# One decoder layer on one core: where the weights lie against the moving rows in two groups of projections, and the order in which the columns are read in a third

## The chip, the core and the metric

The kernel runs on 1 core of one Trainium2 chip (trn2) and is launched once. The metric is the device time of that launch in microseconds. A core has five engines that work side by side: TensorE (PE in the profile, with its weight loads shown apart as PEld), VectorE (DVE), ScalarE (ACT), GpSimd (POOL) and SyncE (SP, which here only starts DMAs). On-chip data lies in SBUF (128 partitions, a long row of bytes in each); a matmul reads both of its operands from SBUF and writes PSUM. Of the two operands, the *stationary* one (here always 128 columns) is loaded first, and the *moving* one (here 256 columns, mostly) is streamed past it.

## The reference

One layer on a sequence of 256 positions with 1024 features, float32 throughout:

```python
proj = x @ w_in + b_in                  # 1024 -> 4*1024 + 8 + 3*1024 + 2*1024 columns
q_m, k_m, v_m, o_m, i_m, f_m, q_b, k_b, v_b, g_a, g_b = split(proj)
q_m, k_m = silu(causal_conv4(q_m, k_m))             # along positions
y_a = sigmoid(o_m) * head_norm(mlstm(q_m, k_m, v_m, i_m, f_m))   # 4 heads x 256
y_b = causal_attention(q_b, k_b, v_b, rel_bias)                  # 8 heads x 128
mix = (sigmoid(g_a) * (y_a @ w_branch_a) + sigmoid(g_b) * (y_b @ w_branch_b)) @ w_out
x = layer_norm(ALPHA * x + mix)
u = causal_conv3(x @ w_up)              # 2 * 2816 columns
x = layer_norm(ALPHA * x + (silu(u_gate) * u_up) @ w_down)
```

## The kernel before

Everything that TensorE multiplies in bulk is float32 split into a high and a low part (type fp32r). A product of two such operands takes three matmuls, `mm3`: high by high, high by low, low by high (lines 125, 126 and 127).

**Steps.** The weights come in 81 chunks of 1 MB (128 partitions by 2048 float32, 8 KB in each partition). `chunk_order` lists them, and the main loop in `run` takes one chunk a step. A step s starts the DMA of chunk s + 5 into a `raw` buffer, splits chunk s + 2 into `wh` and `wl` (`split_into`: a cast on ACT, line 91, and a subtraction on DVE, line 92), and multiplies with chunk s. So the weights of a step are ready two steps ahead, and SyncE's queue holds nothing but the DMAs of chunks and the stores of the output.

**Groups.** Behind four steps for the output gate (`o`) come four groups, 0 to 3, of eight projections each, always in the order qm, qb, km, kb, vm, vb, ga, gb. A projection is one step: 256 columns of `w_in`, 8 slices of 128 in the contraction, 2 halves, 3 matmuls each: 48 matmuls. Between the projections of a group stand the small matmuls of the two branches (their tiles are psw, pss, psl, psn, pst, psy and pso). Then follow `wa`, `wb`, `wo` and the feed-forward part (`up`, `dn`).

**Which operand moves.** In `mm_feat` (qm, qb, km, kb, ga, gb) the weights are stationary, 128 columns at a time, and the 256 positions of x (tiles `xth`, `xtl`: high and low) move. In `mm_tok` (vm, vb, and `o`) it is the other way round: 128 positions of x are stationary, and 256 columns of the weights move.

**Distances.** `wh` and `wl` are views into tiles that are 64 columns wider than the widest chunk needs; `shift` gives the column at which the view begins. "Distance" means here the start of the stationary operand less the start of the moving one, in float32 columns, modulo 64 (256 bytes). The tiles begin at addresses that are equal modulo 512 bytes, and slices follow each other in whole multiples of 128 columns, so a projection has one distance throughout. Before, it is 16 in all 32 projections: the views begin at column 16 where the weights are stationary, at 48 where they move. Three kinds of matmul differ: the very first of each vm, which loads a copy of x with a place of its own (`xfirst`); the first two of the `o` steps (`mm_early`, line 159), which move 512 columns from column 0 of the weight tiles, at distance 0; and the last of the `o` steps (PSUM tiles `ps_o3` and `ps_o3b`), which moves rows of 264 columns (the projection's 256 and 8 for the mLSTM gates), so that the distance falls by 8 from slice to slice and takes each multiple of 8 once.

**Results.** `ps` is a PSUM tile of 2 x 256 columns, which ACT and DVE read in the next step; nothing in this reading depends on the order in which TensorE wrote the columns.

Of the kernel before, what the change touches and what calls it, by code (L numbers as in the profile page):

```python
# [21 lines left out]
KT = D // P  # L22
# [35 lines left out]
    return order  # L58


def shift(kind):

    if kind in ("vm", "vb", "o"):
        return 48
    if kind in ("wa", "wb"):
        return 56
    return 0 if kind in ("wo", "dn") else 16


class Kernel:  # L70
# [27 lines left out]
    def split_parts(self, s):  # L98
        if s >= len(self.order) or s in self.w:
            return []  # L100
        raw = self.raw.pop(s)
        if s in self.extra:
            wh, wl = self.extra.pop(s)
        else:
            wh = self.stream.tile([P, WCOLS], F32R, tag="wh", name=f"wh{s}", bufs=3)
            wl = self.stream.tile([P, WCOLS], F32R, tag="wl", name=f"wl{s}", bufs=3)
            a = shift(self.order[s][0])
            wh, wl = wh[:, a:a + KT * 264], wl[:, a:a + KT * 264]
        if s == 3:

            vh, vl = (t.rearrange("p (k f) -> p k f", k=KT) for t in (wh, wl))
            vr = raw.rearrange("p (k f) -> p k f", k=KT)
            cuts = [tuple(t[:, 4 * i:4 * i + 4, 0:256] for t in (vh, vl, vr)) for i in range(2)]
            cuts.append((vh[:, :, 256:264], vl[:, :, 256:264], self.wif))
        else:
            wh, wl = wh[:, 0:2048], wl[:, 0:2048]
            cuts = [tuple(t[:, i * 1024:(i + 1) * 1024] for t in (wh, wl, raw)) for i in range(2)]
        self.w[s] = (wh, wl)
        return [lambda c=c: self.split_into(*c) for c in cuts]
# [9 lines left out]
    def mm_feat(self, s, ps, xh, xl, mid=None, first=None):  # L129
        wh, wl = self.w.pop(s)  # L130
        wh = wh.rearrange("p (k f) -> p k f", k=KT)
        wl = wl.rearrange("p (k f) -> p k f", k=KT)
        for j in range(2):
            if j and mid:
                mid()
            c = slice(j * P, (j + 1) * P)
            for k in range(KT):
                self.mm3(ps[:, j, :], wh[:, k, c], wl[:, k, c], xh[:, k, :], xl[:, k, :], k == 0, k == KT - 1,
                         first if j == k == 0 else None)

    def mm_tok(self, w, ps, xh, xl, toks=(0, 1), kouter=False, ks=range(KT), first=None):
        wh, wl = w
# [1034 lines left out]
```

## Time and profile before

| | |
|---|---|
| time, median of 2 runs | 498.08 us (497.45 and 498.71) |
| span of the profiled execution, first to last instruction | 495.6 us |
| its own time outside the span | not listed; the median less the span is 2.5 us |
| TensorE busy, its weight loads busy | 484.4 us (98%), 468.0 us (94%) |
| VectorE, ScalarE, GpSimd busy | 369.2 us (74%), 288.5 us (58%), 29.1 us (6%) |
| groups 1, 2 and 3, first matmul of qm to that of the next group | 49.9 us each |
| mean DMA rate | 189 GB/s |

How to read it: the page of a profile describes one execution. Engine times are sums over its instructions; matmuls overlap each other, so a matmul of 276 ns that starts every 113 ns still makes "busy" no more than the span. Rows name the line of the kernel, the engine, the operation, and output <- inputs with the numbers of buffers left out, so `wh` stands for all of its buffers. In a timeline the first column is the start in us from the span's start and the second the duration.

### The profile page before, as it was taken

How to read it: one execution, taken by the hardware profiler on the slowest of the kernel's cores; microseconds unless marked ns; L12 is line 12 of the kernel's file. 1: busy time of each engine (PE TensorE's matmuls, PEld its weight loads, DVE VectorE, ACT ScalarE, POOL GpSimd, SP SyncE). 2: the span in 40 equal slices, each digit the busy share in tenths (PEclk: the TensorE clock that was granted, in tenths of full speed). 3: DMA queues.
4: the chain of work that ended last, by engine and by line, in shares of the span. 5: the costliest groups of instructions: out<-in, count | busy, mean ns of one | idle time of the engine just before them, and what ended most of it. 6: DMA issues, size and time to landing. Idle time of an engine off the chain costs nothing.

```text
span 495.6 us, 9471 instructions
## 1 busy us (share of the span) xinstructions
PE 484.4 (98%) x3889; PEld 468.0 (94%) x3889; DVE 369.2 (74%) x662; ACT 288.5 (58%) x479; POOL 29.1 (6%) x46
## 2 busy tenths in 40 slices
PE   8999999999999999999999999999999999999992
PEld 4899999999999999999999999999999999999982
DVE  5676995888588858885677788888667766866886
ACT  6567867496658665866655524766554555554610
POOL 0400011001100110002000001000000000000001
PEclk9999999999999999999999999999999999999998
DMA  8984555556554645443945572646555456444202
GB/s 251 351 305 153 202 197 200 175 173 193 184 184 171 196 172 196 172 171 136 371 176 179 221 280 86 255 145 212 203 206 175 165 181 245 170 171 171 86 1 85
DMA packets 19036, 93.74 MB, mean 189 GB/s; under 512 B 4625, under 2 KB 5913, under 8 KB 9009
## 3 DMA queue, kind: packets, MB, share of 16 engines
q1 hardware_dynamic: 14834, 87.08, 49.2%
q0 software_dynamic: 4160, 6.07, 3.9%
q8 instruction: 30, 0.49, 0.4%
q14 instruction: 12, 0.10, 0.1%
HBM read 92.05 MB, written 2.63 MB: 191 GB/s over the span
## 4 chain that ended last, share of the span: by engine, by line
PE 94%; DMA 2%; DVE 1%; SPq 1%; ACT 0%; issue 0%; POOL 0%; POOLq 0%
PE ps_up L127 8%; PE ps_up L126 8%; PE ps_up L125 8%; PE ffn L127 4%; PE ffn L126 4%; PE ffn L125 4%; PE ps_vm L125 2%; PE ps_vm L127 2%; PE ps_qm L125 2%; PE ps_vm L126 2%; PE ps_ga L127 1%; PE ps_ga L125 1%; PE ps_vb L126 1%; PE ps_vb L127 1%; PE ps_vb L125 1%; PE ps_ga L126 1%
## 5 line engine op out<-in xcount | busy, mean ns | idle before, releaser
L92 DVE TENSOR_TENSOR wl<-raw,wh 128x1024 fp32r<-128x1024 f32 (+1 forms) x162 | 187.5, 1197 | 29.2 <-ACT wh L91 29.0
L91 ACT CAST wh<-raw 128x1024 fp32r<-128x1024 f32 (+1 forms) x162 | 158.8, 1030 | 11.6 <-DMA raw<-in_wst_dram 6.3
L127 PE MATMUL ps_up<-x1h,wl 128*128 128x256 f32 x320 | 89.9, 281 | 0.0
L126 PE MATMUL ps_up<-x1l,wh 128*128 128x256 f32 x320 | 89.9, 281 | 0.0
L125 PE MATMUL ps_up<-x1h,wh 128*128 128x256 f32 x319 | 89.7, 281 | 0.0
L126 PEld LDWEIGHTS ps_up<-x1l,wh 128*128 128x128 f32 x320 | 61.4, 192 | 0.0
L127 PEld LDWEIGHTS ps_up<-x1h,wl 128*128 128x128 f32 x320 | 60.1, 188 | 0.0
L125 PEld LDWEIGHTS ps_up<-x1h,wh 128*128 128x128 f32 x319 | 59.9, 188 | 0.0
L1010 DVE SCALAR_TENSOR_TENSOR cu<-ps_up,vec,cu 128x255 f32<-128x255 f32 (+1 forms) x80 | 33.0, 475 | 27.1 <-ACT cu L1006 26.9
L127 PE MATMUL ffn<-wh,hl 128*128 128x512 f32 (+1 forms) x110 | 38.4, 349 | 0.0
L126 PE MATMUL ffn<-wl,hh 128*128 128x512 f32 (+1 forms) x110 | 38.4, 349 | 0.0
L125 PE MATMUL ffn<-wh,hh 128*128 128x512 f32 (+1 forms) x110 | 38.3, 349 | 0.0
L91 ACT CAST hh<-cu 128x256 fp32r<-128x256 f32 x22 | 8.9, 407 | 42.8 <-DVE cu L1018 42.8
L1006 ACT ACTIVATE cu<-ps_up,vec 128x256 f32<-128x256 f32 x40 | 16.8, 472 | 28.8 <-PE ps_up L127 28.0
L126 PEld LDWEIGHTS ffn<-wl,hh 128*128 128x128 f32 x110 | 20.8, 189 | 3.0
L125 PEld LDWEIGHTS ffn<-wh,hh 128*128 128x128 f32 x110 | 20.7, 188 | 3.0
L127 PEld LDWEIGHTS ffn<-wh,hl 128*128 128x128 f32 x110 | 20.7, 188 | 2.9
L125 PE MATMUL ps_gb<-xth,wh 128*128 128x256 f32 x64 | 18.0, 282 | 0.0
L126 PE MATMUL ps_vm<-wl,xth 128*128 128x256 f32 x64 | 17.9, 280 | 0.0
L127 PE MATMUL ps_vm<-wh,xtl 128*128 128x256 f32 x64 | 17.9, 280 | 0.0
L125 PE MATMUL mix<-wh,mgh 128*128 128x256 f32 x64 | 17.8, 279 | 0.0
L125 PE MATMUL ps_qm<-xth,wh 128*128 128x256 f32 x64 | 17.8, 278 | 0.0
(295 smaller groups left out, 1428.9 us busy)
## 6 DMA issues: line engine op xcount, KB each, us to landing
raw<-in_wst_dram SPq DMA_DIRECT2D x78, 1024.0 KB, 4.9
raw<-in_wst_dram SPq DMA_DIRECT2D x8, 256.0 KB, 4.5
lnrow<-in_rows_dram POOLq DMA_DIRECT2D x4, 512.0 KB, 7.5
band<-table POOLq DMA_DIRECT2D x4, 384.0 KB, 13.0
xraw<-in_xt_dram SPq DMA_DIRECT2D x8, 128.0 KB, 4.3
raw<-in_wst_dram SPq DMA_DIRECT2D x2, 512.0 KB, 7.6
toe<-band POOLq DMA_DIRECT2D x4, 256.0 KB, 4.2
xtok<-in_x_dram POOLq DMA_DIRECT2D x1, 1024.0 KB, 8.3
```

The costliest lines, as they stand in the source:

```text
L91: self.nc.scalar.copy(wh, raw)
L92: self.nc.vector.tensor_sub(wl, raw, wh.bitcast(F32))
L125: mm(ps, ah if first is None else first, bh, start=start, stop=False)
L126: mm(ps, ah, bl, start=False, stop=False)
L127: mm(ps, al, bh, start=False, stop=stop)
L1006: act.activation(cu[:, j, :], ps[:, j, :], AF.Copy, scale=tap(2, j))
L1010: v.scalar_tensor_tensor(cu[:, j, o:], ps[:, j, :S - o], tap(t, j), cu[:, j, o:], op0=ALU.mult, op1=ALU.add)
```

## The change

The change gives `shift` the group as well. In groups 1 and 3 a table sets the column at which each projection's view begins, and so its distance, for both `wh` and `wl`. Worked out as above, the distances after it are:

| | qm | qb | km | kb | vm | vb | ga | gb |
|---|---|---|---|---|---|---|---|---|
| groups 0 and 2 (and all groups before) | 16 | 16 | 16 | 16 | 16 | 16 | 16 | 16 |
| group 1 | 24 | 20 | 12 | 8 | 24 | 12 | 4 | 0 |
| group 3 | 32 | 40 | 48 | 56 | 0 | 56 | 60 | 18 |

In group 2 the six projections of `mm_feat` stay at 16, but the 256 moving columns are streamed in another order, and the PSUM tile is written in the same order, so each result lands where it did. For qm the order is backwards (255, 254, ... 0). For the others the two halves of the 256 columns alternate in blocks: c columns of the first half, c of the second, c of the first, and so on, with c = 16 (qb), 32 (km), 4 (kb), 64 (ga) and 8 (gb). In the built program each is one matmul as before, with another access pattern.

No instruction is added, removed or moved on any engine. What differs on TensorE is the access patterns of group 2 and the addresses in groups 1 and 3; on ACT and DVE it is the addresses to which the splits of groups 1 and 3 write.

```diff
-def shift(kind):
-
+PLACES = {
+    1: {"qm": 24, "qb": 20, "km": 12, "kb": 8, "vm": 40, "vb": 52, "ga": 4, "gb": 0},
+    3: {"qm": 32, "qb": 40, "km": 48, "kb": 56, "vm": 0, "vb": 8, "ga": 60, "gb": 18},
+}
+READS = {"qm": "back", "qb": 16, "km": 32, "kb": 4, "ga": 64, "gb": 8}
+
+
+def shift(kind, i=0):
+
+    if i in PLACES and kind in PLACES[i]:
+        return PLACES[i][kind]
     if kind in ("vm", "vb", "o"):
         return 48
...
-            a = shift(self.order[s][0])
+            a = shift(*self.order[s])
             wh, wl = wh[:, a:a + KT * 264], wl[:, a:a + KT * 264]
...
+        kind, i = self.order[s]
+        how = READS.get(kind) if i == 2 else None
+
+        def seen(t):
+            if how is None:
+                return t
+            if how == "back":
+                return t[:, ::-1]
+            return t.rearrange("p (a b c) -> p b a c", a=2, c=how)
+
         for j in range(2):
...
-                self.mm3(ps[:, j, :], wh[:, k, c], wl[:, k, c], xh[:, k, :], xl[:, k, :], k == 0, k == KT - 1,
-                         first if j == k == 0 else None)
+                self.mm3(seen(ps[:, j, :]), wh[:, k, c], wl[:, k, c], seen(xh[:, k, :]), seen(xl[:, k, :]), k == 0,
+                         k == KT - 1, first if j == k == 0 else None)
```

## The prediction

> **What bounds the kernel now.** The page comes first, for who is busy and what the chain that ended last consists of.
>
> ```profile
> span 495.6 us, 9471 instructions
> ## 1 busy us (share of the span) xinstructions
> PE 484.4 (98%) x3889; PEld 468.0 (94%) x3889; DVE 369.2 (74%) x662; ACT 288.5 (58%) x479; POOL 29.1 (6%) x46
> ...
> PE 94%; DMA 2%; DVE 1%; SPq 1%; ACT 0%; issue 0%; POOL 0%; POOLq 0%
> ```
>
> TensorE makes 94% of the chain. A busy share says little of pace, since matmuls overlap, so I then asked for the waits of TensorE and for the three groups that change.
>
> ```profile
> PE warm_ps L196 <- DVE warm L193: 1.2, 1, 1.2
> PE ps_o L159 <- ACT wh L91: 0.9, 2, 0.7
> ...
> core 0: us, PE busy (x) PEld busy (x) DVE busy (x) ACT busy (x) POOL busy (x), PEclk, DMA share, GB/s
> 82.80:132.70 49.90, 49.90 (x437) 49.85 (x437) 38.24 (x81) 33.54 (x62) 3.97 (x4) 1.00 0.54 183
> 132.70:182.60 49.90, 49.90 (x437) 49.85 (x436) 38.20 (x81) 33.53 (x62) 3.85 (x4) 1.00 0.53 183
> 182.60:232.50 49.90, 49.90 (x438) 49.85 (x436) 38.24 (x81) 33.54 (x62) 2.04 (x2) 1.00 0.47 169
> ```
>
> The first two rows are the only waits listed for TensorE, both ahead of the groups. Each group takes 49.90 us; TensorE is busy throughout at a granted clock of 1.00, and DVE has 11.7 us and ACT 16.4 us to spare in each. So a group lasts as long as its matmuls stand apart, and one nanosecond on each of the 48 matmuls of a step is 48 ns of kernel time, with nothing to hide it. Four starts give the spacing (the rows are the first matmul of km, kb and vm of group 1, and the first one behind vm).
>
> ```profile
> 93.73 0.28 PE L125 MATMUL ps_km<-xth,wh 128*128 128x256 f32 x1
> ...
> 99.17 0.28 PE L125 MATMUL ps_kb<-xth,wh 128*128 128x256 f32 x1
> ...
> 104.61 0.28 PE L125 MATMUL ps_vm<-wh,xfirst 128*128 128x256 f32 x1
> ...
> 110.27 0.59 PE L603 MATMUL psw<-nM,ident 128*128 128x256 f32 x2
> ```
>
> kb takes 99.17 to 104.61, 5.44 us for 48 matmuls: **113.3 ns** each. vm takes 5.66 us: **117.9 ns** each. Now the durations by tile (least, median, most in ns); one row of three for each projection, all four groups together.
>
> ```profile
> L92 DVE TENSOR_TENSOR wl<-raw,wh x65: 1189/1218/1246, 30.3 to 231.1; 128x1024 fp32r<-128x1024 f32 x65
> ...
> L127 PE MATMUL ps_qm<-xth,wl x64: 276/276/281, 32.0 to 188.0; 128*128 128x256 f32 x64
> ...
> L127 PE MATMUL ps_qb<-xth,wl x64: 276/276/276, 37.9 to 193.4; 128*128 128x256 f32 x64
> ...
> L127 PE MATMUL ps_km<-xth,wl x64: 276/276/276, 43.3 to 198.8; 128*128 128x256 f32 x64
> ...
> L127 PE MATMUL ps_kb<-xth,wl x64: 276/276/276, 48.8 to 204.3; 128*128 128x256 f32 x64
> ...
> L126 PE MATMUL ps_vm<-wl,xth x64: 276/281/284, 54.6 to 209.8; 128*128 128x256 f32 x64
> ...
> L126 PE MATMUL ps_vb<-wl,xth x64: 276/276/281, 62.3 to 217.4; 128*128 128x256 f32 x64
> ...
> L127 PE MATMUL ps_ga<-xth,wl x64: 276/276/285, 69.7 to 224.7; 128*128 128x256 f32 x64
> ...
> L127 PE MATMUL ps_gb<-xth,wl x64: 276/276/283, 76.0 to 230.8; 128*128 128x256 f32 x64
> ```
>
> Duration less spacing is 276 - 113.3 = 162.7 for kb and 281 - 117.9 = 163.1 for vm. So a duration, less 163, reads as a spacing. 276 is the least that any of these rows shows and the median of seven projections; vm stands at 281. Both are at distance 16, so the distance alone does not fix the pace: there are two, and a step falls into one of them.
>
> **The change, part by part.** No instruction comes, goes or moves; what can change is the pace of 16 + 6 steps.
>
> *Groups 1 and 3, other distances.* 14 of these 16 steps (all but vm) now run at 113.3: 14 x 48 = 672 matmuls; vm's 96 run at 117.9. The trace has few matmuls at other distances. The nearest are the last chunk of the output gate, whose 264 columns pass through every multiple of 8, and the first two chunks, 512 columns at distance 0; beside these stands the same width at distance 16 in the feed-forward part (512 and 256 columns mixed, the median is one of 512).
>
> ```profile
> L125 PE MATMUL ps_o<-wh,xth x8: 282/284/286, 25.0 to 27.6; 128*128 128x264 f32 x8
> ...
> L126 PE MATMUL ps_o<-wl,xth x8: 278/283/287, 25.1 to 27.7; 128*128 128x264 f32 x8
> ```
>
> ```profile
> L125 PE MATMUL ps_o3b<-wh,xth x8: 281/282/290, 27.9 to 30.5; 128*128 128x264 f32 x8
> ```
>
> ```profile
> L159 PE MATMUL ps_o<-wh,xth x8: 389/389/796, 5.9 to 16.8; 128*128 128x512 f32 x8
> ```
>
> ```profile
> L125 PE MATMUL ffn<-wh,hh x71: 276/392/398, 340.1 to 469.6; 128*128 128x512 f32 x43, 128*128 128x256 f32 x28
> ```
>
> 512 columns at distance 0: 389 - 163 = 226, twice 113.3 within a rounding. So 113.3 per 256 columns is the undisturbed pace, met at distance 0 as well as at 16. At distance 16 the same width shows 392 and up to 398, 3 to 9 ns more: the distance of 16 is no guarantee, and 0 no penalty. For 264 columns the undisturbed duration would be 163 + 113.3 x 264/256 = 280; the rows have medians of 282 to 284 (2 to 4 more), a least of 278 and a most of 290 (10 more). So a matmul at another distance costs between 0 and 10 ns over the pace; the vm rows, of the right width and steady over 48 matmuls, say 4.6. I take **4.6 ns**, as the 264-column rows lie nearer to it than to either end, for all 672: 672 x 4.6 = **+3.1 us**; vm, already there, 0. Bounds: below, all 672 keep their pace and vm reaches it, -96 x 4.6 = -0.4 us; above, all 768 pay 10 over the pace, of which vm's 96 pay about 5 already: 672 x 10 + 96 x 5 = +7.2 us.
>
> [...]
>
> *Group 2, other orders.* Six steps, 288 matmuls at 113.3. Nothing in the trace reads or writes columns out of order, so the price is bounded by rows for columns in order. Below: 0, since 256 and 512 columns show the same least pace per column, that of a stream with nothing in its way; no order can need fewer columns. Above: a column that takes two places in the stream, as if there were 512 of them; 389 - 276 = 113 ns on each matmul, 48 x 113 = 5.4 us for a step and 32.6 us for six. [...] 288 x 4.6 = **+1.3 us**.
>
> *What hides beside it.* The splits write to other columns of the same tiles. The row of DVE above holds halves written at columns 16, 48 and 56; they differ by 57 ns at most, and 16 such halves in a group would add 0.9 us to an engine with 11.7 us to spare. ACT and DVE read PSUM in its old layout one step later. If TensorE slows, their margin and that of the chunk DMAs grows. The small matmuls between the projections keep their operands; what the projection before them leaves changes at most their first one or two (most of 281 to 285 against 276: up to 9 ns, some 0.1 us in all, left out).
>
> *Sum.* Span 495.6 + 3.1 + 1.3 = 500.0 us; the profiled execution's time outside the span isn't shown, and I take the 2.5 us by which the median of the two runs exceeds the span: **502.5 us**, 0.9% over the median of 498.1. Two per cent, 10 us, is about what a measurement of this kernel can tell from no change, so this is "the same".
>
> **The rivals.**
>
> *Distance decides nothing.* For it: 389 at distance 0, 276 and 281 at one distance, least values of 278 at mixed ones. Against it: the 264-column medians all lie above 280. Then only group 2 pays: 498.1 + 1.3 = 499.4 us; if its steps keep their pace too and vm gains, 497.7.
>
> *The worst price of a distance throughout.* Every matmul of groups 1 and 3 pays the most seen, 290: 498.1 + 7.2 + 1.3 = 506.6 us. Against it: one row in the list reaches it, once.
>
> *Backwards runs at half pace.* [...] 3.1 + 5 x 48 x 4.6 ns (1.1) + 5.4 = 9.6: 507.7 us. Nothing in the trace speaks for or against.
>
> *Slower: every broken order at half pace.* The mechanism is one place, the stream of group 2: if moving columns or PSUM columns that aren't neighbours cost a place of their own, the six steps pay up to 32.6 us: 498.1 + 3.1 + 32.6 = 533.8 us. It decides from 24 ns a matmul on (10 - 3.1 = 6.9 us over 288). Against it: blocks of 4 to 64 columns break the order at one column in 4 at most, so that half pace needs more than a break's own cost. [...]
>
> *Not as described.* That the views and patterns don't end up as the tables say would leave 498.1; the tables in the change were worked out from the built program's addresses, so I give this nothing of its own.
>
> **How the numbers follow.** Forecast, 502.5: 0.50 (with its own range of 500.3 to 504.7, half of the two terms either way). Distance decides nothing: 0.22. Worst price throughout: 0.07. Backwards at half pace: 0.14. Every order at half pace: 0.07. The range of 8 in 10: below, it takes in the second case but for its end, 497.9; above, the backwards case with a share of its neighbours' prices, 510. Left out are the last case (0.07), the ends of the two before it (0.04) and of the second (0.05). Over 2% slower, from 508.0 on, are the last case, a third of the backwards one and a little of the worst price: 0.14. Over 2% faster would need 10 us, and no row gives more than 0.4: 0.01. The same: 0.85.
>
> **What would show it.** In the changed profile the durations by tile tell each step: 281 in place of 276 for the 14 steps; 276 there would mean case two, 286 and above the worst price. The windows of groups 1 and 3 should grow from 49.90 to about 51.4 us, that of group 2 to about 51.2, and group 0 and everything behind group 3 should keep its length. For orders, ps_qm's most tells: 276 or 281 as forecast, near 389 for half pace; kb and gb, with the shortest blocks, come next. The prediction is wrong if one step of group 2 alone takes over 2 us more, if distances cost more than 10 ns or differ so much that a mean hides it, or if a pace once fallen into is carried on into steps that did not change.

## The result, and the profile after

The changed kernel takes **502.87 us** (502.73 and 503.01), before 498.08; the ratio is 1.0101 with a 95% interval of 1.0072 to 1.013. So it is slower by 1.0%, within the 2% that count as the same and clear of the noise of these runs. The span of the profiled execution grew from 495.6 to 501.0 us.

First the span, then the three groups, each from the first matmul of its qm to that of the next group (of the last one: to the first of `wa`). Columns as before: length, busy time of the engines, granted clock, DMA.

```profile
span 501.0 us, 9475 instructions
```

The four instructions more than the 9471 before are semaphore instructions, three in TensorE's queue and one in VectorE's, so the change did add something. They come with the orders, not with the distances, and they are no part of the loss that shows: in the run with reads and writes apart, further down, they stand in a group that keeps its old pace (kb at 276). Matmuls and weight loads are 3889 each, as before.

```profile
82.69:134.29 51.60, 51.60 (x437) 51.55 (x436) 38.25 (x81) 33.52 (x62) 3.93 (x4) 1.00 0.53 177
134.29:186.27 51.98, 51.98 (x438) 51.93 (x436) 38.24 (x81) 33.58 (x62) 3.85 (x4) 1.00 0.51 176
186.27:237.89 51.62, 51.62 (x438) 51.57 (x437) 38.26 (x81) 33.53 (x62) 2.04 (x2) 1.00 0.45 164
```

The groups took 49.87, 49.89 and 49.89 us with the bounds set in the same way, so they grew by 1.73, 2.09 and 1.73 us, 5.55 in all; the span grew by 5.4, as group 1 begins 0.16 us earlier now. VectorE's and ScalarE's busy times and the clock are what they were. The loss is TensorE's, inside the three groups.

Next the matmuls by projection in each group (least, median, most duration in ns; less 163 that is the spacing, within some 1.5 ns). First group 1, one row of three for qb and kb and all three of km.

```profile
L134 PE MATMUL ps_qb<-xth,wh x16: 278/280/282, 88.4 to 93.7; 128*128 128x256 f32 x16
...
L134 PE MATMUL ps_km<-xth,wh x16: 278/278/278, 94.1 to 99.4; 128*128 128x256 f32 x16
L135 PE MATMUL ps_km<-xtl,wh x16: 280/280/280, 94.2 to 99.5; 128*128 128x256 f32 x16
L136 PE MATMUL ps_km<-xth,wl x16: 282/282/284, 94.3 to 99.6; 128*128 128x256 f32 x16
...
L134 PE MATMUL ps_kb<-xth,wh x16: 277/280/285, 99.7 to 105.1; 128*128 128x256 f32 x16
```

No row of group 1 has the old 276 as its median any more, and the durations no longer agree with each other: in km each of the three matmuls of a slice has one of its own, in kb they run through 277 to 285. The starts show a repeating cycle: in qm of group 1 the spacings are, behind the first few, 117, 119, 122, 120, 115 and again from the start, give or take 1 ns. Group 2, with qm, with kb and gb as the dearest orders, and with vm and vb, which did not change:

```profile
L134 PE MATMUL ps_qm<-xth,wh x16: 278/279/279, 134.3 to 139.6; 128*128 128x256 f32 x16
L135 PE MATMUL ps_qm<-xtl,wh x16: 282/282/282, 134.4 to 139.7; 128*128 128x256 f32 x16
...
L134 PE MATMUL ps_kb<-xth,wh x16: 286/290/298, 151.4 to 157.1; 128*128 128x256 f32 x16
...
L135 PE MATMUL ps_vm<-wl,xth x16: 276/276/278, 157.6 to 162.7; 128*128 128x256 f32 x16
...
L134 PE MATMUL ps_vb<-wh,xth x16: 281/281/281, 165.1 to 170.4; 128*128 128x256 f32 x16
...
L135 PE MATMUL ps_gb<-xtl,wh x16: 284/286/288, 178.9 to 184.4; 128*128 128x256 f32 x16
```

kb, read in blocks of 4, is the worst. And vm and vb have changed places: vm went from 281 to 276, vb from 276 to 281, though nothing in them differs. Mean spacings in ns, worked out from the starts (48 matmuls each, gb with one wait of some 200 ns at its head in every version):

| | qm | qb | km | kb | vm | vb | ga | gb |
|---|---|---|---|---|---|---|---|---|
| before, groups 1 to 3 | 113.5-113.7 | 113.3 | 113.3 | 113.3 | 117.8 | 113.6 | 113.7 | 115.5 |
| group 1 after | 118.8 | 118.6 | 117.7 | 118.4 | 117.4 | 119.2 | 118.4 | 121.6 |
| group 2 after | 117.7 | 120.0 | 118.8 | 126.9 | 113.6 | 117.8 | 117.8 | 125.1 |
| group 3 after | 118.6 | 119.8 | 117.8 | 117.8 | 119.8 | 116.8 | 120.0 | 120.1 |

### The profile page after: what moved, and what is told of

It is laid out like the page before. It is cut to its first block, busy times and chain, and to the rows that moved or that the text cites. A ratio compares the mean times of both kernels' runs of the same rounds, so it can differ in the third digit from the quotient of the medians.

```text
span 501.0 us, 9475 instructions
## 1 busy us (share of the span) xinstructions
PE 489.8 (98%) x3889; PEld 473.5 (94%) x3889; DVE 370.1 (74%) x662; ACT 288.7 (58%) x479; POOL 30.8 (6%) x46
## 4 chain that ended last, share of the span: by engine, by line
PE 94%; DMA 3%; DVE 1%; ACT 0%; POOL 0%; issue 0%; SPq 0%; POOLq 0%
PE ps_up L136 8%; PE ps_up L134 8%; PE ps_up L135 8%; PE ffn L136 4%; PE ffn L135 4%; PE ffn L134 4%; DMA raw<-in_wst_dram 3%; PE ps_qm L134 2%; PE ps_gb L134 2%; PE ps_kb L136 2%; PE ps_vm L134 2%; PE ps_kb L134 2%; PE ps_kb L135 2%; PE ps_gb L136 2%; PE ps_ga L134 2%; PE ps_ga L136 2%
## 5 line engine op out<-in xcount | busy, mean ns | idle before, releaser
L134 PE MATMUL ps_kb<-xth,wh 128*128 128x256 f32 x64 | 18.1, 282 | 0.0
L135 PE MATMUL ps_kb<-xtl,wh 128*128 128x256 f32 x64 | 18.1, 282 | 0.0
L134 PE MATMUL ps_qb<-xth,wh 128*128 128x256 f32 x64 | 18.0, 282 | 0.0
L136 PE MATMUL ps_kb<-xth,wl 128*128 128x256 f32 x64 | 18.0, 282 | 0.0
```

What stands on the lines that cost most here:

```text
L134: mm(ps, ah if first is None else first, bh, start=start, stop=False)
L135: mm(ps, ah, bl, start=False, stop=False)
L136: mm(ps, al, bh, start=False, stop=stop)
```

## The experiments

Two theories of the distances stood against each other at first. **A:** a distance has a pace of its own. **B:** what counts is the way into a step, that is, from what neighbour the stream comes. A third, **C**, came up for the alignment of the operands by themselves.

**One part at a time.** The two parts of the change alone:

```diff
-READS = {"qm": "back", "qb": 16, "km": 32, "kb": 4, "ga": 64, "gb": 8}
+READS = {}            # the first run; the second instead: PLACES = {}
```

> Only the other distances of groups 1 and 3; group 2 reads in order as before. Theory A (each distance other than 16 keeps weight loads and moving rows in each other's way in a repeating cycle): groups 1 and 3 take 51.6 us each as in the changed kernel, group 2 goes back to 49.9, total +3.4 us, about 501.5 us. Theory B (what counts is how a step enters, that is, that neighbours differ): the same total here. Rival (loss comes from the orders and is carried on into group 3): groups 1 and 3 near 50, total under 499.5 us.

> Only the other orders of group 2; all distances 16. Theory A: group 2 takes 52.0 us as in the changed kernel, the others 49.9, total +2.1 us, about 500.2 us; with the distances alone the two losses add up to that of the changed kernel. Rival (a pace fallen into is carried on): group 3, unchanged here, also slower than 49.9 us.

Measured: the distances alone 501.59 us against 498.31 (ratio 1.0062, 1.0045 to 1.0079), the orders alone 499.94 against the same 498.31 (1.0038, 1.0023 to 1.0053). The three groups, for the distances and then for the orders:

```profile
83.43:135.03 51.60, 51.60 (x437) 1.00 0.53 177
135.03:184.91 49.88, 49.88 (x438) 1.00 0.54 183
184.91:236.53 51.62, 51.62 (x438) 1.00 0.45 164
```

```profile
83.13:133.00 49.87, 49.87 (x437) 1.00 0.53 183
133.00:184.95 51.95, 51.95 (x437) 1.00 0.52 176
184.95:234.83 49.88, 49.88 (x437) 1.00 0.46 169
```

Each part costs what it costs in the changed kernel, and a group that is left alone keeps its 49.9 us. The losses add, and no group's loss reaches the next one.

**Reading or writing.** In `mm_feat` of the kernel with the orders alone, in groups 1 to 3:

```diff
...
+                out = ps[:, j, :] if i == 1 else seen(ps[:, j, :])
+                bh, bl = (t[:, k, :] if i == 3 else seen(t[:, k, :]) for t in (xh, xl))
...
```

> All distances 16. The orders of group 2 are used in three groups, but in group 1 only the moving rows are read in that order and PSUM is written in order (so the positions of q, k and the gates are permuted there, and the output isn't the reference's), in group 2 both as in the changed kernel, in group 3 only PSUM is written in that order (permuted too). If the price is on the reading side: group 1 shows kb +13.6 ns a matmul, gb +9.7, qb +6.7, km +5.5, ga and qm +4.5 over 113.3, as group 2 does, and group 3 shows 113.3 throughout. If it is on the writing side: the other way round. If either breaks the stream: both show it.

Measured: one row of kb for each group, by tile: group 1 reads in blocks of 4 and writes in order, group 2 does both, group 3 reads in order and writes in blocks of 4.

```profile
L131 PE MATMUL ps_kb<-xth,wh x16: 286/290/298, 100.4 to 106.1; 128*128 128x256 f32 x16
```

```profile
L131 PE MATMUL ps_kb<-xth,wh x16: 286/290/298, 152.4 to 158.1; 128*128 128x256 f32 x16
```

```profile
L131 PE MATMUL ps_kb<-xth,wh x16: 276/276/276, 203.6 to 208.7; 128*128 128x256 f32 x16
```

The price is on the reading side, whole. By the mean spacings group 1 repeats group 2 in all eight projections (117.7, 120.0, 118.8, 126.9, 113.6, 117.8, 117.8, 125.1), and group 3 that of before (113.3 to 113.7, vm 117.8, gb 115.5). So writing PSUM backwards or in blocks of 4 to 64 neighbours cost nothing here.

**One distance per group.** From the kernel before:

```diff
+EVEN = {1: 0, 2: 32, 3: 8}
+UPS = {2: 0, 3: 8, 4: 24, 5: 32, 6: 40, 7: 48, 8: 56, 9: 4, 10: 12}
...
+    if kind in ("qm", "qb", "km", "kb", "ga", "gb") and i in EVEN:
+        return EVEN[i]
+    if kind == "up" and i // 2 in UPS:
+        return UPS[i // 2]
```

> Reading in order everywhere. The six projections with stationary weights have one distance per group: 0 in group 1, 32 in group 2, 8 in group 3; the up steps of the feed-forward part have 0 to 56 by pairs (0, 8, 24, 32, 40, 48, 56, 4, 12 for up 4-5 to 20-21), before 16 throughout. Theory A: every step at another distance than 16 stays at 117 to 122 ns a matmul in a cycle of its own, also where the step ahead has the same distance: groups 1 to 3 about 51.4 us each. Theory B (entry decides): in groups 1 to 3 the steps behind a step of the same distance (qb, km, kb) run at 113.3, groups about 50. For up, which is at 117.8 with distance 16: by A 117 to 122 at each distance; any distance that shows 113.3 there would make a faster kernel.

Measured: 503.44 us, one run. Steps whose neighbour has the same distance are not faster: qb, km and kb stand at 120.0 in group 1 (distance 0), 118.6 to 118.7 in group 2 (32), 118.3 in group 3 (8). B, as stated, falls: a step at these distances is slow behind a neighbour of the same distance too. In `up` the means are 120.0, 118.3, 120.0, 118.7, 119.9, **113.3**, 116.6, 118.4 and 117.8 for the distances 0, 8, 24, 32, 40, 48, 56, 4 and 12. First `up` 4, at 0, then `up` 14, at 48; before, all of these stood at 281.

```profile
L133 PE MATMUL ps_up<-x1h,wh x16: 283/283/283, 334.4 to 339.8; 128*128 128x256 f32 x16
```

```profile
L133 PE MATMUL ps_up<-x1h,wh x16: 276/276/276, 419.6 to 424.7; 128*128 128x256 f32 x16
```

But 48 was in the changed kernel too, in km of group 3, at 117.8. So 48, like 16, shows two paces. Nor does A hold to the letter for the others: 24 ran at 118.8 in qm and 117.4 in vm of the changed kernel, and at 120.0 in `up`. At 0 the spacing settles within some ten matmuls at 120 ns throughout, as it does in `up` at 24; at the rest, 48 aside, it runs in cycles (in kb durations of 279 to 285 at 32, of 277 to 285 at 8).

**The operands by themselves.** x's tiles and the weights of all projections moved by the same 8 columns, with all distances kept:

```diff
-        xth = mp.tile([P, KT, S], F32R, name="xth")
-        xtl = mp.tile([P, KT, S], F32R, name="xtl")
+        xt2 = mp.tile([P, 32 + 2 * KT * S], F32R, name="xt2")[:, 8:8 + 2 * KT * S]
+        xt2 = xt2.rearrange("p (w k s) -> p w k s", w=2, k=KT)
+        xth, xtl = xt2[:, 0], xt2[:, 1]
...
```

> x's high and low tiles and the weights of the 32 projections all begin 8 columns (32 bytes) further on, so every distance stays 16. Theory A (the distance between the two streams counts): every projection keeps its pace, qm to kb at 113.3 ns a matmul, vm at 117.9, groups 49.9 us, total within 0.5 us of before. Theory C (where an operand lies against 64 or 256 bytes counts): the projections run at 117 to 122 as at the distances 8 and 24, groups 51 to 52 us, total +5 us.

Measured: 498.94 us against 498.07, one run. C falls: none of the cycles at 118 to 120 appears. Yet A is not the whole of it: qm to kb went to a steady 117.8 in groups 2 and 3 and stayed at 113.3 in groups 0 and 1 (but for qm of group 0, which went to 117.8 too), while vm went the other way in groups 2 and 3. One row, qm of group 2, of the steady kind:

```profile
L129 PE MATMUL ps_qm<-xt,wl x16: 281/281/281, 132.9 to 138.2; 128*128 128x256 f32 x16
```

Same distance, same alignment in all four groups, and two paces. The kernel before has this already: vm is at 276 in group 0 and at 281 in the other three, and vb and ga the other way round. That leaves the way into a step, but as **B'**: at distance 16 (and 48) there are two steady paces, 113.3 and 117.8, and the way in decides between them; at 256 columns no other distance tried reaches the faster one (the lowest mean, 116.6, is that of `up` at 56).

**Disturb the first matmuls.** From the kernel before, the first one to three matmuls of a step read and write in another order:

```diff
+KICKS = {("up", 4 + i): (n, how) for i, (n, how) in enumerate((n, h) for n in (1, 2, 3) for h in ("back", 4, 8, 16, 32, 64))}
+KICKS |= {("vm", 1): (1, 4), ("vm", 2): (2, 4), ("vm", 3): (3, 4)}
...
+            if self.kick and self.kick[0]:
+                p, b = (turned(t, self.kick[1]) for t in (p, b))
+                self.kick = self.kick[0] - 1, self.kick[1]
```

> All distances 16; in up 4 to 21 the first one, two or three matmuls read and write their columns backwards or in alternating blocks of 4, 8, 16, 32 or 64 (18 steps, one combination each), and in vm of groups 1, 2, 3 the first one, two, three in blocks of 4; all else as before. Theory B' (at distance 16 there are two steady paces, 113.3 and 117.8, and the way in decides which): some of these steps change from 117.8 to 113.3 for all of their remaining 45 to 47 matmuls, vm of group 2 of the changed kernel having done so behind a step in blocks of 4. Rival (what the step is decides: up and vm run at 117.8 by their operands): all stay at 117.8, and the turned matmuls cost 1 to 13 ns each.

Measured: 498.02 us against 498.07, and both outcomes side by side. Of the 18 steps of `up` ten end at 113.3 for all that is left of them and eight stay at 117.8; of vm all three change. In the rows stand `up` 7, whose first matmul is in blocks of 16; `up` 9, the same with blocks of 64; then vm of group 2 with two matmuls in blocks of 4, and vb and ga behind it, untouched.

```profile
L140 PE MATMUL ps_up<-x1l,wh x17: 276/276/283, 352.4 to 357.9; 128*128 128x256 f32 x17
```

```profile
L140 PE MATMUL ps_up<-x1l,wh x17: 281/281/281, 369.1 to 374.7; 128*128 128x256 f32 x17
```

```profile
L140 PE MATMUL ps_vm<-wl,xth x16: 276/276/290, 155.7 to 160.8; 128*128 128x256 f32 x16
```

```profile
L140 PE MATMUL ps_vb<-wh,xth x16: 281/281/281, 163.2 to 168.5; 128*128 128x256 f32 x16
```

```profile
L140 PE MATMUL ps_ga<-xtl,wh x16: 281/281/281, 170.6 to 175.9; 128*128 128x256 f32 x16
```

One matmul out of order set the pace of nearly all of the 47 behind it, 276 as the median in `up` 7: B' holds. It did so in `up` 4, 6 and 7 and in vm of group 1, and not in `up` 5, 8 and 9; these runs show no rule for it, and do not separate the order from the few ns that it costs. `up` 21, directly behind `up` 20 at 113.3, ran at that pace from its first matmul on, though its first three were in blocks of 64: there, with no other matmul between, the pace went over to the next step. Those three stand 113 to 114 ns apart, so blocks of 64 cost nothing in themselves there. And vb, behind a faster vm, is at 281, as in the changed kernel: the exchange of vm and vb there needs no order or distance of their own. ga behind it stands at 117.8 in groups 1 to 3, read in order, which is what it shows in blocks of 64 in group 2 of the changed kernel.

**Distance 48.** From the kernel before, `up` at 48 and vm of groups 1 to 3 at 48; then `up` at 48 with the down projection's distances varied instead of vm's:

```diff
+    if kind == "up":
+        return 48
+    if kind == "vm" and i:     # the second run instead: if kind == "dn" and i < 8: return 8 * i
+        return 16
```

> up 2 to 21 at distance 48 (before 16) and vm of groups 1 to 3 at distance 48; all else as before. In the run with even distances up 14 and 15 showed 113.3 at 48. If 48 holds there for every up: 20 x 48 x 4.5 ns = 4.3 us less; vm, 3 x 48 x 4.5 = 0.6 us less if it does the same: about 493.4 us. Rival (the way in decided there too, since the steps ahead differed): only some steps gain, 495.5 to 498.

> up at distance 48 as in the run before; the down projection's steps dn 0 to dn 7 at distance 16, 8, 0, 56, 48, 40, 32, 24, its last three at 16 (before 16 throughout). By theory A each distance has a pace of its own: at 512 columns 226.7 ns (as the first two output gate chunks at distance 0) to 236; dn 2 at 0 or dn 4 at 48 would be fastest. Rival (widths of 512 and 256 follow each other there and keep the streams out of step at any distance): all eight steps within 1% of each other.

Measured: the first 493.95 us against 498.07 (ratio 0.9917, 0.99 to 0.9933). `up` 4 to 21 stand at 113.3, `up` 3 and vm at 117.8, so vm gave nothing and `up` all of it: 18 x 48 x 4.5 ns = 3.9 us. The second, one run, 498.48 us: `up` 4 and 5, still behind the unchanged distance, at 113.3, and all from `up` 6 on at 117.7 to 117.9. So 48 is no better than 16; it has the same two paces, 113.3 and 117.8, and the steps ahead decide. The same step, `up` 8, in the first run and in the second (there the window ends behind 12 of its 16 matmuls):

```profile
L129 PE MATMUL ps_up<-x1h,wh x16: 276/276/276, 362.1 to 367.2; 128*128 128x256 f32 x16
```

```profile
L129 PE MATMUL ps_up<-x1h,wh x12: 279/279/279, 363.4 to 367.3; 128*128 128x256 f32 x12
```

In the second the three matmuls of a slice have durations of their own, of which this row is one; the spacings from the starts average 117.8.

The down projection itself hardly minds: at distance 0 its 512-column matmuls fall from 232.7 to 229.1 ns and its 256-column ones rise from 116.0 to 118.7, which is 18 x 3.6 - 12 x 2.7 = 32 ns a step; the eight distances lie within 1.6% of each other, by the sum over a step. The rival of that run, which said 1%, was nearly right.

**Orders, without the jump.** From the kernel with the orders alone, all six projections of a group in one order, with neighbouring blocks exchanged in place of blocks from two halves (backwards in group 3):

```diff
-        how = READS.get(kind) if i == 2 else None
+        how = {1: 4, 2: 16, 3: "back"}.get(i) if kind in READS else None
...
-            return t.rearrange("p (a b c) -> p b a c", a=2, c=how)
+            return t.rearrange("p (b a c) -> p b a c", a=2, c=how)[:, :, ::-1, :]
```

> All distances 16; all six projections with stationary weights of a group read and write in one order: blocks of 4 with each two neighbours exchanged (4-7, 0-3, 12-15, 8-11, ...) in group 1, blocks of 16 exchanged in group 2, backwards in group 3. If each break of the order has a price wherever the next block lies: 126.9 ns a matmul in group 1 (as kb in the changed kernel, blocks of 4 taken from two halves), 120.0 in group 2 (as its qb), 117.7 in group 3. Rival (the price comes from the jump of 128 columns between the halves): groups 1 and 2 under 119.

Measured: 501.88 us, one run. Neither answer fits all: blocks of 16 cost 120.0, as from two halves, but blocks of 4 cost 117.7 in place of 126.9. kb of group 1 (blocks of 4) and of group 2 (blocks of 16):

```profile
L131 PE MATMUL ps_kb<-xth,wh x16: 278/278/278, 99.8 to 105.1; 128*128 128x256 f32 x16
```

```profile
L131 PE MATMUL ps_kb<-xth,wh x16: 284/284/284, 151.3 to 156.7; 128*128 128x256 f32 x16
```

So it is not the number of breaks (63 in a matmul in blocks of 4). Blocks of 4 are dear, at 126.9, where each one lies 128 columns (512 bytes) from the last; exchanged within 32 bytes they cost what a run backwards costs (117.7 to 117.8). Why is open.

**A version that beats both.** `up` at 48, and the first matmul of vm, vb and ga turned:

```diff
+KICKS = {("vm", g): (1, 4) for g in (1, 2, 3)}
+KICKS |= {(n, g): (1, (4, 4, "back", 8)[g]) for n in ("vb", "ga") for g in range(4)}
+KICKS[("up", 3)] = (1, "back")
...
+    if kind == "up":
+        return 48
```

> up 2 to 21 at distance 48, and the first matmul of vm (groups 1 to 3), of vb and ga (all groups) and of up 3 turned (blocks of 4, backwards or blocks of 8, by group). By theory B' (two steady paces at distance 16, the way in decides): up gains 18 x 48 x 4.5 ns = 3.9 us as in the run with up and vm at 48, vm of groups 1 to 3 and vb and ga of group 0 go from 117.8 to 113.3 (5 x 0.2 us), the other vb and ga keep 113.3: about 493 us. Rival (a turned matmul throws a step into one pace or the other as it falls): some vb and ga end at 117.8, which costs 0.2 us each; 493.5 to 495.

Measured: **492.86 us** against 497.38 for the kernel before on that chip (15 runs from 493.9 to 499.3), ratio 0.9914 (0.9889 to 0.994): 0.9% faster, within the 2% that count as the same and clear of the noise of these runs. The span is 490.8 us. vm of the last three groups, and vb of all four:

```profile
L143 PE MATMUL ps_vm<-wl,xth x48: 276/276/286, 104.4 to 208.9; 128*128 128x256 f32 x48
```

```profile
L143 PE MATMUL ps_vb<-wh,xth x64: 276/276/288, 62.2 to 216.4; 128*128 128x256 f32 x64
```

Every projection of the groups now has a median spacing of 113; `up` 2 and 3 stayed at 117.8 and 117.7, as at distance 16, so the turned matmul of `up` 3 did nothing for it; `up` 0 and 1 stayed at 117.5 and 113.8. Of its gain over the kernel before, 3.9 us are `up`'s; against the run with `up` and vm at 48 the span is 1.2 us shorter, 0.3 of it ahead of group 0; the remaining 0.9 is near the 1.0 forecast for vm, vb and ga.

## Why the prediction was right, and where it was not

- **What bounds the kernel, and that nothing hides a nanosecond on a matmul**: right. Three groups at 100% TensorE, other engines' busy time unchanged, and the sum of the groups' growth (5.55 us) is about that of the span (5.4).
- **Groups 1 and 3, +3.1 us**: 3.46, at 5.0 ns in place of 4.6 on average over the 14 steps (3.1 for vb of group 3, 6.4 for its qb). vm, put at 0, went from 117.8 to 117.4 and to 119.8. The row it was taken from, vm at 281, named the size and not the thing: vm's pace is the second steady one of distance 16, while the other distances run in cycles, or at 120.0, that happen to average about the same. So this term was met in part by luck. "0 no penalty", read from 512 columns, does not carry over to 256: with one distance per group they stand at 120.0 there, 6.7 over the pace. The rows of 264 columns, medians 2 to 4 over the pace, were the better witness for what the change does.
- **Group 2, +1.3 us**: 2.09, and this is the term that was mis-sized: 7.2 ns on average in place of 4.6. One price for all orders was wrong. No run shows 4.6 ns as the price of an order, which was the author's choice; in its place the runs showed, over the spacing before, 4.0 ns for qm, 6.7 for qb, 5.5 for km, 13.5 for kb, 4.0 for ga and 9.6 for gb. Only ga left the good pace for the other steady one, 117.8, and its order need not be the reason: read in order behind vb at 117.8, with the first matmuls of vm turned, ga stood there too.
- **A pace carried into steps that did not change** was named as something that would make the prediction wrong. Something near it happened: vm and vb of group 2 changed pace, set by the way in, and cancelled by luck, -4.2 and +4.2 ns on 48 matmuls each.
- **Time outside the span**, taken as 2.5 us: this was the median of two runs, which differ by 1.3 us, less the span of a single execution. Wherever time and span of one run are on record they are 1.7 to 2.1 us apart (2.0 in the profiled run of the changed kernel). The two terms together came out 1.1 us above the forecast, and the median is 1.9 over the span now, 0.6 less than was taken; that the total, 502.87 for 502.5, is closer than its parts is luck.
- **Rivals.** *Distance decides nothing*: refuted by the distances alone (1.0062, above 1 with its whole interval) and by one distance per group (qb, km and kb at 120.0, 118.6 to 118.7 and 118.3, before 113.3). *Backwards at half pace*: 117.7, no. *Every order at half pace*: the dearest order costs 12%, and all of it on the reading side. *Worst price throughout*: single matmuls of groups 1 and 3 reach 285 to 288, no step there averages more than 6.4 over its old spacing.

Why the place of one operand against the other, or the order of the columns, changes the pace was not shown: a row gives the start and the duration of a matmul, and no cause. What fixes the choice between the two steady paces, why 16 and 48 reach 113.3 at 256 columns and the other distances tried do not (116.6 at the lowest), stays open.

## What to carry to other kernels

Where TensorE is the bound and its matmuls are short (here busy for 98% of the span, one start every 113 to 118 ns), read the least duration of a shape in the whole trace and compare every step with it: two steps of the same shape at 276 and 281 ns were 4% apart here (spacings of 113.3 and 117.8), and TensorE's list of waits had no row for the groups. Then try the place of the operands in SBUF, and a disturbance at a step's head, step by step in one kernel, since here the pace of a step hung on what ran ahead of it: `up` 8, at distance 48 in both runs, stood at 113.3 in one and at 117.8 in the other.

## What was not expected of the hardware

- At distance 16 a stream of equal matmuls had two steady spacings, 113.3 and 117.8 ns (vm, vb and ga of the kernel before, each in both), and one matmul with its columns in another order put those behind it from the slower into the faster in `up` 4, 6 and 7 and in vm of group 1.
- At most other distances the spacing ran through a fixed cycle (near 117, 119, 122, 120, 115 ns in qm of group 1, at distance 24); at distance 0 it settled at 120 ns.
- In the run with reads and writes apart, writing PSUM backwards or in blocks of 4 to 64 columns cost nothing (kb at 276 throughout, mean spacings as before); in the changed kernel, reading the moving rows backwards or in blocks of 4 to 32 taken from two halves cost 4.0 to 13.5 ns on 113.3.
